# Handing a layer's token mixer to its channel mixer: the last tile by halves of 512, its neighbour turned inside the last product, the written order begun one tile earlier, and 13 sums a layer on GpSimd

## The chip, the cores and the metric

One core of a Trainium2 chip runs the whole kernel. The metric is device time in microseconds. The core has TensorE (PE; its weight loads are listed as PEld), VectorE (DVE), ScalarE (ACT), GpSimd (POOL) and SyncE (SP, which issues the transfers). A program runs one queue of instructions on each engine, and the engines wait for each other through semaphores.

## The reference

Two layers of an encoder over 1024 tokens of 1024 channels, all in float32. Cut to what matters here:

```python
def rms_norm(x, g):
    return x * rsqrt(mean(x * x, -1) + EPS) * g

def conv_glu_ffn(h, w_in, conv_w, conv_b, w_out):      # D_FF = 2816
    gate, val = split(h @ w_in, 2, -1)
    gate = conv over tokens, 3 taps, per channel (gate) + conv_b
    return (gelu(gate) * val) @ w_out

# layer i
y = mixer_i(rms_norm(x, g0))           # attention of the layer, ending in o @ w_o
x = x + rms_norm(o @ w_o, g1)          # g1: norm of the mixer's output
f = conv_glu_ffn(rms_norm(x, g2), ...)
x = x + rms_norm(f, g3)
x = x + gated embedding (x, p[i], g4)
```

Layer 0's mixer is a neighbourhood attention over 16 x 64 tokens, layer 1's a dense differential attention. The places that change are the two at which `o @ w_o` ends and `h @ w_in` begins.

## The kernel before

**Products in float32.** An operand is split into a high part (a rounding copy, `high`, by ScalarE, line 249) and a low part (what is left, `low`, by VectorE, line 252). A product of two operands is then three matmuls into one sum bank (`mm3`, lines 286 to 288): high by high, low weight by high, high weight by low.

**The mixer's last product.** `mix_out` goes over eight tiles of 128 tokens in the order 0, 4, 1, 5, 2, 3, 6, 7. For each tile it multiplies by w_o (48 matmuls, line 1392: eight blocks of 128 channels, two halves of 512 output channels, three matmuls each), and then:

- ScalarE squares the two halves of the result (1551), VectorE adds the two sums (1555), GpSimd raises the mean to the power -1/2 (298: "the root"), VectorE scales by the root and g1 (1561: "the residual") and adds x (1564);
- ScalarE squares the new x (293), GpSimd takes the second root (298), and VectorE scales by it and g2 (306, for the last tile 1605: "the norm");
- TensorE turns the tile (eight transposes, 317), and the parts are stored for the channel mixer.

The names below call the last four tiles c = 2, d = 3, a = 6 and b = 7. Tiles 0 to 3 are one half of the tokens and 4 to 7 the other.

**The channel mixer.** `h @ w_in` is worked in 22 blocks of output channels. A block's 2 x 2 product is formed in seven products instead of eight (the operands are named A for weights, B for tokens, S and T for their sums): one = A11 B11, six = S2 T2, two = A12 B21, three = S3 T3, five = S1 T1, four = A22 T4, seven = S4 B22. A product is twelve matmuls, and the results are summed by VectorE (`upper`, 1785, is one of these sums) and GpSimd (`upper_on`, 1788). The token sums are made per tile while it is turned: T1 = B12 - B11 (`sum_t1`, 1496), T2 = B22 - T1 (`sum_t2`, 1500), T3 = B22 - B12 (`sum_t3`, 1504) and T4 = B21 - T2 (`sum_t4`, 1508). The weights come as raw pages, and their sums S1 to S4 (`sum`, 1746; for the first two blocks lines 75 and 79) are made by VectorE up to block 4, from block 5 on by GpSimd. After every second block four sums Z (1914 to 1917) of the gated result are made by VectorE, for the product by w_out, and written out.

**The order.** The scheduler orders ScalarE and VectorE up to tile a. From the last tile on, to the end of the third block, their order is the written one (`manual_schedule`, ending after `first_three`); TensorE runs as written throughout. The last product does three of its eight channel blocks, then turns tile d, then does the other five; behind it stand tile a's transposes, block 0's `one`, block 1's `one`, `two` of block 0, tile b's transposes, `two` of block 1, and then `six`. `Begun` holds what blocks 0 and 1 need before the last token tile is there.

Of the kernel before, what the change touches and what calls it, by code (L numbers as in the profile page):

```python
# [40 lines left out]
class Begun:  # L41


    def __init__(self, trunk, layer, X):
        self.trunk, self.layer, self.X = trunk, layer, X
        self.A = [trunk.weights_of(layer, 0)]
        self.o = [{k: trunk.operand(self.A[0][k]) for k in ("A11", "A12")}, {}]
        self.begun = []

    def weight(self, f, k):  # L50
        self.o[f][k] = self.trunk.operand(self.A[f][k])

    def weights(self):
# [152 lines left out]
class Trunk:  # L206
# [1229 lines left out]
    def mix_out(self, layer, x_in, x1):  # L1436
# [9 lines left out]
        with ExitStack() as pools:  # L1446
            x = pools.enter_context(self.tc.tile_pool(name=f"xb{layer}", bufs=2, reuse_waits="tile"))
            if layer == 0:
                self.ps = pools.enter_context(self.psum("s", 2))
            else:  # L1450
                pools.push(self.spool)
# [77 lines left out]
            def product_of(n, t, amid=None):  # L1529
                hi, lo, xi = ready.pop(0)  # L1530
                part = [(hi[:, k], lo[:, k]) for k in range(KT)]
                if t == 0 or layer == 1 and n == 1:
                    m = (self.out1 if n else self.out0)[2]
                    self.times(m, part[KT - 1 :], W[KT - 1 :], first=False)
                else:
                    m = self.ps.tile([P, D], F32, tag="s", name=self.uid("m"))
                    m = [m[:, :512], m[:, 512:]]
                    if amid is None:
                        self.times(m, part, W)
                    else:  # L1540
                        for _ in self.times_steps(m, part[:3], W[:3], last=False):
                            pass
                        amid()
                        self.times(m, part[3:], W[3:], first=False)
                return m, xi

            def squares(m, h):
                ss = [self.col("ss"), self.col("sy")]
                for half in range(2):
                    w = slice(half * 512, half * 512 + 512)  # L1550
                    nc.scalar.activation(h[:, w], m[half], AF.Square, scale=D**-0.5, accum_out=ss[half])
                return ss
# [31 lines left out]
            m, xi = product_of(NT - 1, b, lambda: self.transposed(hs[-2], put(order[-3], hs[-2])))  # L1584
            h = self.page(x, "h")
            hs.append(h)
            (a1, a2), (b1, b2) = sums(hs[-2]), sums(h)
            ss = squares(m, h)
# [3 lines left out]
            gate.weights()  # L1592
            self.high(grid(ps[1]), of(b22, a))
            self.high(grid(ps[0]), of(b12, a))
            gate.one(0)
            residual(b, m, h, xi, r)
            self.split(a1, *both("T1", a))
            gate.copy(0)
            gate.one(1)
            sum_t2(a, a1, a2)  # L1600
            gate.weight(1, "A12")
            r = self.rstd(xi, h)
            gate.copy(1)
            gate.sum1(0), gate.sum2(0)
            nc.vector.scalar_tensor_tensor(out=h, in0=xi, scalar=r, in1=g2, op0=ALU.mult, op1=ALU.mult)
            s2 = gate.high(0, 1)
            self.high(a2, both("T2", a)[0])
            gate.low(0, 1, s2)
            gate.two(0)
# [61 lines left out]
    def product(self, ps, o, X, first):  # L1671
        for k in range(4):
            self.mm3(ps, (o[:, 0, k], o[:, 1, k]), (X[:, 0, k], X[:, 1, k]), first and k == 0, k == 3, not first)
# [4 lines left out]
    def gated(self, layer, X, spill, spare):  # L1678
# [38 lines left out]
        with self.tc.tile_pool(name=f"xd{layer}", bufs=1, reuse_waits="tile") as y, self.psum("c", 2) as pc:  # L1717
# [7 lines left out]
            class Block:  # L1725
# [33 lines left out]
                def product(b, ps, a, x, first):  # L1759
                    self.product(ps, b.o[a], X[x], first)  # L1760
# [8 lines left out]
                def six(b):  # L1769
                    b.product(b.pc, "S2", "T2", True)  # L1770
# [44 lines left out]
            def first_three():  # L1815
# [3 lines left out]
                b0.six()  # L1819
# [49 lines left out]
                b2.copy()  # L1869
                b0.gelu()  # L1870
                b2.centre(0)
                b0.mult((1,))
                b2.three(), b2.upper(), b2.upper_on(pool)
                b0.mult((0,))
                b1.taps(1)
# [4 lines left out]
                return b0, b1, b2  # L1880
# [3 lines left out]
            for f in range(FT):  # L1884
                if f < 3:
                    b = begun[f]
                else:
                    b = Block(f)
                    b.part("A11")
                    for s in ("S1", "S2", "S3", "S4"):  # L1890
                        b.sum(s, tt if f < 5 else pool)
                    b.part("S2", "A12", "S1", "S3", "S4", "A22")
# [21 lines left out]
                tt(out=Z[:, 0], in0=even[:, t2], in1=c[:, t2], op=add)  # L1914
                tt(out=Z[:, 1], in0=Z[:, 0], in1=even[:, t1], op=sub)
                tt(out=Z[:, 2], in0=even[:, t1], in1=even[:, t2], op=sub)
                tt(out=Z[:, 3], in0=c[:, t1], in1=Z[:, 1], op=sub)
# [502 lines left out]
```

## Time and profile before

| | |
|---|---|
| median of three runs | 2681.57 us (2681.15 to 2682.80) |
| the profiled execution | 2682.3 us, its span 2680.5 us |
| TensorE clock granted | 0.999 |
| busy PE, PEld | 2656.7 us (99%), 2198.9 us (82%) |
| busy DVE, ACT, POOL | 1964.7 us (73%), 1385.2 us (52%), 554.4 us (21%) |
| handover of layer 0, layer 1 | about 535 to 660 us, 1933 to 2057 us |

Rows of the timeline read: start, duration, engine, line, operation, output<-inputs, the shape, how many instructions were joined; in brackets the idle time before it and what ended it. In rows of windows a stretch is followed by each engine's busy time and count. Matmuls overlap by their pipeline, so two starts tell more than one duration.

### The profile page before, as it was taken

What the parts mean: (1) busy time and instruction counts of PE and PEld (TensorE: products, weight loads), DVE (VectorE), ACT (ScalarE), POOL (GpSimd) and SP (SyncE); (2) the same over time, 40 slices, a digit from 0 to 9 for tenths busy, and PEclk for the clock granted to TensorE, in tenths of its full rate; (3) what the DMA queues carried; (4) which work ended last, traced back from release to release, by engine and by line L of the source; (5) the groups of instructions that cost most, each with busy time, mean ns of one, the idle gap of its engine ahead of it and who ended that gap; (6) DMA issues with size and microseconds to landing.
All of it is one profiled execution on the core that took longest, in us unless ns stands there. A gap on an engine that the chain in (4) does not pass through costs nothing.

```text
span 2680.5 us, 37056 instructions
## 1 busy us (share of the span) xinstructions
PE 2656.7 (99%) x13428; PEld 2198.9 (82%) x13428; DVE 1964.7 (73%) x3369; ACT 1385.2 (52%) x2615; POOL 554.4 (21%) x528
## 2 busy tenths in 40 slices
PE   8999999999999999999999999999999999999999
PEld 7888887878888888888878888887878888888887
DVE  5777777699777778676587777775798777768674
ACT  5565556354444444454466666676454343444452
POOL 3221220003343300001442121210103433300000
PEclk9999999999999999999999999999999999999999
DMA  6323225523323274343346555553414232373443
GB/s 177 94 66 105 78 90 190 137 71 126 118 95 114 87 275 146 102 141 110 118 165 210 199 184 196 179 187 100 155 66 141 84 118 95 121 253 133 118 132 108
DMA packets 151081, 360.91 MB, mean 135 GB/s; under 512 B 14153, under 2 KB 41289, under 8 KB 150898
## 3 DMA queue, kind: packets, MB, share of 16 engines
q1 hardware_dynamic: 150898, 358.56, 40.9%
q8 instruction: 105, 1.72, 0.3%
q14 instruction: 78, 0.64, 0.1%
HBM read 277.79 MB, written 92.90 MB: 138 GB/s over the span
## 4 chain that ended last, share of the span: by engine, by line
PE 91%; DVE 4%; ACT 2%; issue 1%; DMA 1%; POOL 1%; SPq 0%; ACTq 0%; DVEq 0%; POOLq 0%
PE b L286 20%; PE b L288 20%; PE b L287 20%; PE m L1392 5%; PE g L1392 5%; PE b L1146 4%; PE s L1088 4%; PE b L1132 2%; PE b L1392 2%; PE b L317 2%; PE av L981 2%; PE b L954 1%; PE s L935 1%; PE s L934 1%; DVE r L252 1%
## 5 line engine op out<-in xcount | busy, mean ns | idle before, releaser
L286 PE MATMUL b<-r,ws 128*128 128x512 f32 x1244 | 512.8, 412 | 0.0
L288 PE MATMUL b<-r,ws 128*128 128x512 f32 x1244 | 487.4, 392 | 0.4 <-DVE ws L252 0.4
L287 PE MATMUL b<-r,ws 128*128 128x512 f32 x1244 | 486.7, 391 | 0.5 <-DVE r L252 0.5
L288 PEld LDWEIGHTS b<-r,ws 128*128 128x128 f32 x1244 | 233.5, 188 | 52.9 <-DVE ws L252 1.3
L298 POOL TENSOR_TENSOR ss<-ss,mhalf 128x1 f32<-128x1 f32 x128 | 77.7, 608 | 944.6 <-DVE ss L1150 416.4
L286 PEld LDWEIGHTS b<-r,ws 128*128 128x128 f32 x1244 | 234.1, 188 | 45.4 <-issue 2.9
L286 PE MATMUL b<-r,wa 128*128 128x512 f32 x688 | 268.0, 390 | 2.0 <-DVE B L1785 2.0
L288 PE MATMUL b<-r,wa 128*128 128x512 f32 x688 | 268.0, 389 | 0.0
L287 PE MATMUL b<-r,wa 128*128 128x512 f32 x688 | 267.7, 389 | 0.0
L287 PEld LDWEIGHTS b<-r,ws 128*128 128x128 f32 x1244 | 234.9, 189 | 34.7 <-DVE r L252 1.4
L286 PE MATMUL b<-r,r 128*128 128x512 f32 x648 | 254.4, 393 | 1.1 <-ACT ws L2161 0.6
L287 PE MATMUL b<-r,r 128*128 128x512 f32 x648 | 252.9, 390 | 0.0
L288 PE MATMUL b<-r,r 128*128 128x512 f32 x648 | 252.4, 390 | 0.0
L249 ACT ACTIVATE r<-raw 128x512 fp32r<-128x512 f32 (+1 forms) x168 | 108.8, 655 | 193.6 <-PE b L287 170.1
L252 DVE TENSOR_TENSOR ws<-raw,ws 128x512 fp32r<-128x512 f32 (+3 forms) x177 | 171.4, 974 | 47.1 <-ACT ws L249 45.4
L1102 DVE CUSTOM_DVE_ANT_0 E<-s,T 128x1024 f32<-128x1024 f32 x128 | 155.7, 1218 | 33.7 <-PE s L1088 32.9
L249 ACT ACTIVATE ws<-raw 128x512 fp32r<-128x512 f32 (+3 forms) x177 | 122.4, 698 | 110.3 <-PE b L288 51.9
L252 DVE TENSOR_TENSOR r<-raw,r 128x512 fp32r<-128x512 f32 (+1 forms) x168 | 125.1, 749 | 70.5 <-ACT r L249 66.3
L1392 PE MATMUL m<-r,ws 128*128 128x512 f32 x672 | 157.5, 392 | 0.0
L286 PEld LDWEIGHTS b<-r,wa 128*128 128x128 f32 x688 | 129.2, 188 | 29.9 <-DVE B L1785 3.3
L288 PEld LDWEIGHTS b<-r,wa 128*128 128x128 f32 x688 | 129.1, 188 | 27.8 <-DVE wa L252 1.0
L1109 ACT ACTIVATE E<-E,mn 128x1024 f32<-128x1024 f32 x128 | 146.9, 1148 | 9.6 <-DVE mn L1102 8.2
(235 smaller groups left out, 5528.1 us busy)
## 6 DMA issues: line engine op xcount, KB each, us to landing
r<-stashT SPq DMA_DIRECT2D x108, 512.0 KB, 4.9
raw<-in_w_in SPq DMA_DIRECT2D x86, 512.0 KB, 3.5
raw<-in_qkv SPq DMA_DIRECT2D x48, 512.0 KB, 4.3
spillS<-r SPq DMA_DIRECT2D x88, 256.0 KB, 3.2
r<-in_ffn_w_out SPq DMA_DIRECT2D x40, 512.0 KB, 6.2
raw<-spillS SPq DMA_DIRECT2D x40, 512.0 KB, 3.5
spillA<-B SPq DMA_DIRECT2D x66, 256.0 KB, 3.0
raw<-spillA SPq DMA_DIRECT2D x30, 512.0 KB, 3.7
```

The source lines that it names most:

```text
L249: return self.nc.scalar.activation(hi, src, AF.Copy).ins
L252: return self.nc.vector.tensor_tensor(out=lo, in0=src, in1=hi.bitcast(F32), op=ALU.subtract).ins
L286: mm(out, sta[0], mov[0], start=first, stop=False, skip_group_check=onto)
L287: mm(out, sta[0], mov[1], start=False, stop=False, skip_group_check=onto)
L288: mm(out, sta[1], mov[0], start=False, stop=last, skip_group_check=onto)
L298: self.nc.gpsimd.tensor_tensor(out=ss, in0=ss, in1=self.mhalf, op=ALU.pow)
L317: self.nc.tensor.transpose(t[:, k * P : k * P + P], h[:, c : c + P], self.ident)
L1088: nc.tensor.matmul(s[m][:, w], A[o, a, q], A[o, b, w], start=z == 0, stop=z == 2)
L1102: self.nc.vector.tensor_tensor_reduce(out=e, in0=s, in1=bias, scale=1.0, scalar=3e38, op0=ALU.add, op1=ALU.min, accum_out=mn)
L1109: self.exp = self.nc.scalar.activation(e, e, AF.Exp, bias=mn, scale=-1.0, accum_out=sm).ins
L1146: nc.tensor.matmul(o, wT[:, k], V[:, k], start=k == 0, stop=k == KT - 1)
L1392: mm(out[half], a, b[:, w], start=first and k + z == 0, stop=last and k == n - 1 and z == 2)
```

## The change

For each layer:

1. **Tiles.** The norms of tiles d and a, and the whole work of tiles a and b, come into the written order, which now also holds GpSimd. The last product is in steps: three channel blocks, tile d's transposes, one channel block, blocks 5 to 8 of half 0, blocks 5 and 6 of half 1, tile a's transposes, blocks 7 and 8 of half 1. Each half has a sum bank of its own; in layer 1 the fourth product takes the banks named `pj`.
2. **Halves.** Tile b's residual, addition, second square and norm are each done in halves of 512 channels.
3. **Weights.** Block 0's A11 and block 1's A12 are opened (high part) early and closed (low part) later; S1 and S2 of block 0 are summed, and A12 split, during the last product; block 3's A11, S1, S2 and A12 are worked inside `first_three`.
4. **GpSimd.** Five token sums (`sum_t2` of a, `sum_t3` of both, `sum_t4` of both) and the eight Z sums of blocks 1 and 3 go from VectorE to GpSimd.
5. **six.** Block 0's `six` does its eight matmuls with the high token part first, the four with the low part last.

The core of the diff:

```diff
-            for n, t in enumerate(order[:-1]):
+            for n, t in enumerate(order[:-2]):
...
-                self.normed(xi, h, g2)
-                if n + 2 < NT:
-                    ready.append(load(order[n + 2]))
+                if n < NT - 3:
+                    self.normed(xi, h, g2)
+                ready.append(load(order[n + 2]))
...
-            self.region = self.tc.manual_schedule(engines={ENG.Activation, ENG.DVE})
+            self.region = self.tc.manual_schedule(engines={ENG.Activation, ENG.DVE, ENG.Pool})
...
+            m, xb, steps = last_product(b)
+            steps(0, 3)
+            ps = [self.turned(hs[-2], g) for g in range(2)]
+            hs.append(self.page(x, "h"))
+            steps(3, 4)
...
+            r = self.rstd(xa, h)
+            self.low(grid(ps[1]), *both("B21", d))
+            gate.weights()
+            steps(4, 8, 0)
+            ss = [self.col("ss"), self.col("sy")]
+            square(m[0], hs[-1], 0, ss)
+            norm(h, xa, r, slice(0, D))
+            gate.sum1(0)
+            gate.sum2(0)
+            gate.weight(0, "A12")
+            steps(4, 6, 1)
+            ps = [self.turned(h, g) for g in range(2)]
+            steps(6, 8, 1)
...
+            square(m[1], h, 1, ss)
             sum_t1(a, ps[0], a1)
             r = root_of(ss)
...
+            sum_t2(a, a1, a2, pool)
...
+            for n, w in enumerate(halves):
+                nc.vector.scalar_tensor_tensor(
+                    out=h[:, w], in0=m[n], scalar=r, in1=g1[:, w], op0=ALU.mult, op1=ALU.mult
+                )
+                tt(out=xb[:, w], in0=h[:, w], in1=xb[:, w], op=ALU.add)
+                if n == 0:
+                    s2 = gate.high(0, 1)
+                square(xb[:, w], h, n, sy)
...
+            r = root_of(sy)
             gate.one(1)
+            gate.copy(1)
+            gate.close(1, "A12", A12)
+            gate.two(0)
+            sum_t3(a, pool)
+            norm(h, xb, r, halves[0]), norm(h, xb, r, halves[1])
             self.high(a2, both("T2", a)[0])
-            gate.low(0, 1, s2)
-            gate.two(0)
             ps = [self.turned(h, g) for g in range(2)]
             gate.two(1)
             sum_t1(b, ps[0], b1)
             self.high(grid(ps[1]), of(b22, b))
             self.high(grid(ps[0]), of(b12, b))
+            sum_t3(b, pool)
             sum_t2(b, b1, b2)
+            self.high(b2, both("T2", b)[0])
             self.low(a2, *both("T2", a))
-            self.split(b2, *both("T2", b))
+            self.low(b2, *both("T2", b))
+            self.split(a1, *both("T1", a))
             self.split(b1, *both("T1", b))
...
-                sum_t4(a, a2), sum_t4(b, b2)
-
-            sum_t3(a), sum_t3(b)
+                sum_t4(a, a2, pool), sum_t4(b, b2, pool)
...
+        if late:
+            steps = [(a, k, 0) for k in range(4) for a in (0, 1)] + [(0, k, 1) for k in range(4)]
...
-                b0.six()
+                b0.six(True)
...
+                b3 = Block(3)
+                b3.part("A11")
...
+                tz = pool if f < 4 else tt
+                tz(out=Z[:, 0], in0=even[:, t2], in1=c[:, t2], op=add)
```

How the order moves, in layer 0 (numbers tell one page or bank from another).

TensorE, the end of the last product. `m` is the sum before, `b_1037` half 1 of it after; `h_5537` and `h_5543` are tile a. Before:

```order
L1392 MATMUL m_5565<-r_896_4687,ws_5466 128x512 x2
L317 MATMUL b_1038_5634<-ident,h_5537 128x128 x4
L317 MATMUL b_1039_5639<-ident,h_5537 128x128 x4
L286 MATMUL b_1043_5657<-r_945_4957,ws_5557 128x512
L287 MATMUL b_1043_5657<-r_945_4957,ws_5557 128x512
```

After:

```order
L326 MATMUL b_1047_5640<-ident,h_5543 128x128 x4
L326 MATMUL b_1048_5645<-ident,h_5543 128x128 x4
L1401 MATMUL b_1037_5563<-r_896_4687,ws_5465 128x512
L1401 MATMUL b_1037_5563<-r_897_4688,ws_5465 128x512
L1401 MATMUL b_1037_5563<-r_896_4687,ws_5466 128x512
L1401 MATMUL b_1037_5563<-r_896_4687,ws_5465 128x512
L1401 MATMUL b_1037_5563<-r_897_4688,ws_5465 128x512
L1401 MATMUL b_1037_5563<-r_896_4687,ws_5466 128x512
L295 MATMUL b_1049_5662<-r_945_4957,ws_5560 128x512
```

Tile a's eight transposes moved ahead of the last six matmuls.

GpSimd, up to block 0's `upper_on` (before: both roots of tile a, both of tile b; after: those of tile b). `B_950`, `B_951` and `B_952` are the tokens' B12, B21 and B22, `h_5543` holds tile a's T2, `h_5592` tile b's. Before:

```order
L298 TENSOR_TENSOR ss_5538<-ss_5538,mhalf 128x1
L298 TENSOR_TENSOR ss_5548<-ss_5548,mhalf 128x1
L298 TENSOR_TENSOR ss_5630<-ss_5630,mhalf 128x1
L298 TENSOR_TENSOR ss_5694<-ss_5694,mhalf 128x1
L1788 TENSOR_TENSOR B_950_4970<-B_950_4970,c_1081_5996 128x512
```

After:

```order
L307 TENSOR_TENSOR ss_5625<-ss_5625,mhalf 128x1
L1506 TENSOR_TENSOR h_5543<-B_952_4972,h_5543 128x512
L307 TENSOR_TENSOR ss_5680<-ss_5680,mhalf 128x1
L1510 TENSOR_TENSOR B_950_4970<-B_952_4972,B_950_4970 128x64x8 x2
L1514 TENSOR_TENSOR B_951_4971<-B_951_4971,h_5543 128x64x8
L1514 TENSOR_TENSOR B_951_4971<-B_951_4971,h_5592 128x64x8
L1869 TENSOR_TENSOR B_950_4970<-B_950_4970,c_1089_6007 128x512
```

Five sums now stand between and behind the two roots, the first `sum_t3` (line 1510, joined with tile b's) right behind the second root.

VectorE, behind tile b's transposes: T2, the lows of T2, T1 and S1, and then the sums T3 and T4. `r_946` is T2, `r_948` T1, `r_945` B11, `ws` are weights. Before:

```order
L1500 TENSOR_TENSOR h_5629<-B_952_4972,h_5629 128x512
L252 TENSOR_TENSOR r_946_4958<-h_5537,r_946_4958 128x64x8
L252 TENSOR_TENSOR r_946_4958<-h_5629,r_946_4958 128x64x8
L252 TENSOR_TENSOR r_948_4960<-h_5629,r_948_4960 128x64x8
L252 TENSOR_TENSOR ws_5750<-r_1040_5648,ws_5750 128x512
L75 TENSOR_TENSOR r_1040_5648<-r_1040_5648 128x512
L79 TENSOR_TENSOR r_1040_5648<-r_1040_5648,raw_5649 128x512
L252 TENSOR_TENSOR ws_5755<-r_1040_5648,ws_5755 128x512
L252 TENSOR_TENSOR ws_5758<-r_1040_5648,ws_5758 128x512
L1504 TENSOR_TENSOR B_950_4970<-B_952_4972,B_950_4970 128x64x8 x2
L1508 TENSOR_TENSOR B_951_4971<-B_951_4971,h_5537 128x64x8
L1508 TENSOR_TENSOR B_951_4971<-B_951_4971,h_5629 128x64x8
```

After, from tile b's norm:

```order
L1608 SCALAR_TENSOR_TENSOR h_5592<-x_5471,ss_5680,g_959_4987 128x512 x2
L1502 TENSOR_TENSOR h_5592<-b_1056_5728,r_945_4957 128x512
L1502 TENSOR_TENSOR h_5592<-h_5592,r_945_4957 128x512
L1506 TENSOR_TENSOR h_5592<-B_952_4972,h_5592 128x512
L261 TENSOR_TENSOR r_946_4958<-h_5543,r_946_4958 128x64x8
L261 TENSOR_TENSOR r_946_4958<-h_5592,r_946_4958 128x64x8
L261 TENSOR_TENSOR r_948_4960<-h_5543,r_948_4960 128x64x8
L261 TENSOR_TENSOR r_948_4960<-h_5592,r_948_4960 128x64x8
L261 TENSOR_TENSOR ws_5763<-r_1042_5609,ws_5763 128x512
```

Tile a's low of T1 has come in ahead of S1's low (`ws`), and the sums of lines 1504 and 1508 have gone to GpSimd. The norm is two instructions.

More of the change, by code (lines that the diff above doesn't have):

```diff
@@ L1534, in product_of, with last_product, steps, square @@
                     self.times(m, part[KT - 1 :], W[KT - 1 :], first=False)
-                else:
+                elif layer == 1 and n == 2:
                     m = self.ps.tile([P, D], F32, tag="s", name=self.uid("m"))
                     m = [m[:, :512], m[:, 512:]]
[L1538 to L1544, printed above, removed]
-                return m, xi
+                    self.times(m, part, W)
+                else:
+                    m = [self.bank(sums_of) for _ in range(2)]
+                    self.times(m, part, W)
+                return m, xi
+            def last_product(t):
+                hi, lo, xi = ready.pop(0)
+                part = [(hi[:, k], lo[:, k]) for k in range(KT)]
+                m = [self.bank(sums_of) for _ in range(2)]
+                def steps(k0, k1, half=None):
+                    out, mov = m, W[k0:k1]
+                    if half is not None:
+                        w = slice(half * 512, half * 512 + 512)
+                        out, mov = m[half : half + 1], [(wh[:, w], wl[:, w]) for wh, wl in mov]
+                    for _ in self.times_steps(out, part[k0:k1], mov, k0 == 0, k1 == KT):
+                        pass
+                return m, xi, steps
+            def square(src, h, half, ss):
+                w = slice(half * 512, half * 512 + 512)
+                nc.scalar.activation(h[:, w], src, AF.Square, scale=D**-0.5, accum_out=ss[half])
             def squares(m, h):
@@ L1549, in squares @@
                 for half in range(2):
[L1550 to L1551 removed]
+                    square(m[half], h, half, ss)
                 return ss
@@ L1582, in mix_out @@
             self.region.__enter__()
-            a, b = order[-2:]
[L1584 to L1588, printed above, removed]
-            ps = [self.turned(hs[-2], g) for g in range(2)]
+            pool = nc.gpsimd.tensor_tensor
+            norm = lambda h, xi, r, w: nc.vector.scalar_tensor_tensor(
+                out=h[:, w], in0=xi[:, w], scalar=r, in1=g2[:, w], op0=ALU.mult, op1=ALU.mult
+            )
@@ new lines, in mix_out @@
+            halves = slice(0, 512), slice(512, 1024)
+            a, b = order[-2:]
+            c, d = order[-4:-2]
+            r = self.rstd(xi, h)
+            m, xa = product_of(NT - 2, a)
+            ps = [self.turned(hs[-2], g) for g in range(2)]
+            hs.append(self.page(x, "h"))
+            for g in range(2):
+                self.high(grid(ps[g]), both(("B11", "B21")[g], c)[0])
+            self.low(grid(ps[0]), *both("B11", c))
+            norm(h, xi, r, slice(0, D))
+            h = hs[-1]
@@ new lines, in mix_out @@
+            r = root_of(squares(m, h))
+            self.low(grid(ps[1]), *both("B21", c))
+            self.high(grid(ps[1]), of(b21, c))
+            residual(a, m, h, xa, r)
+            A11 = gate.open(0, "A11")
+            m, xb, steps = last_product(b)
+            steps(0, 3)
+            ps = [self.turned(hs[-2], g) for g in range(2)]
+            hs.append(self.page(x, "h"))
+            steps(3, 4)
+            for g in range(2):
+                self.high(grid(ps[g]), both(("B11", "B21")[g], d)[0])
@@ L1669, in operand, with product @@
         return o
-    def product(self, ps, o, X, first):
+    def product(self, ps, o, X, first, late=False):
+        if late:
+            steps = [(a, k, 0) for k in range(4) for a in (0, 1)] + [(0, k, 1) for k in range(4)]
+            for n, (a, k, b) in enumerate(steps):
+                self.nc.tensor.matmul(
+                    ps, o[:, a, k], X[:, b, k], start=first and n == 0, stop=n == 11, skip_group_check=not first
+                )
+            return
         for k in range(4):
```

93 lines of the change are left out of this document (53 added, 40 removed).

## The prediction

> **What bounds the kernel now.** I read the page's busy times first, then the waits of TensorE, then the two handovers (product w_o into channel mixer) row by row.
>
> ```profile
> PE 2656.7 (99%) x13428; PEld 2198.9 (82%) x13428; DVE 1964.7 (73%) x3369; ACT 1385.2 (52%) x2615; POOL 554.4 (21%) x528
> ```
>
> TensorE is the bound, and the change leaves its matmuls as many as they were, so only its gaps can move. The view of waits, TensorE alone (total, times, longest, us), has four rows for the handovers:
>
> ```profile
> PE b L317 <- DVE h L1605: 2.4, 2, 1.2
> PE b L286 <- DVE B L1785: 2.0, 3, 1.2
> PE b L287 <- DVE r L252: 0.5, 2, 0.2
> PE b L317 <- ACT B L249: 0.3, 2, 0.2
> ```
>
> That is 5.2 us in nine waits, over two layers. The timeline of layer 0's handover shows where they stand (start, us, engine, line, out<-in, count, idle and releaser):
>
> ```profile
> 540.59 0.60 PE L317 MATMUL b<-ident,h 128*128 128x128 f32 x4
> 541.34 0.66 PE L317 MATMUL b<-ident,h 128*128 128x128 f32 x4 [0.15 <-ACT B L249]
> 541.76 7.07 PE L1392 MATMUL m<-r,ws 128*128 128x512 f32 x30
> 548.83 1.06 PE L317 MATMUL b<-ident,h 128*128 128x128 f32 x8
> ...
> 557.71 0.39 PE L288 MATMUL b<-r,ws 128*128 128x512 f32 x1
> 559.29 1.06 PE L317 MATMUL b<-ident,h 128*128 128x128 f32 x8 [1.19 <-DVE h L1605]
> 560.11 0.48 PE L286 MATMUL b<-r,ws 128*128 128x512 f32 x1
> ...
> 562.95 0.44 PE L286 MATMUL b<-r,ws 128*128 128x512 f32 x1
> 563.61 0.50 PE L287 MATMUL b<-r,ws 128*128 128x512 f32 x1 [0.22 <-DVE r L252]
> 626.16 0.39 PE L288 MATMUL b<-r,wa 128*128 128x512 f32 x1
> 626.83 0.50 PE L286 MATMUL b<-r,wa 128*128 128x512 f32 x1 [0.29 <-DVE B L1785]
> 645.78 0.39 PE L288 MATMUL b<-r,wa 128*128 128x512 f32 x1
> 647.33 0.50 PE L286 MATMUL b<-r,wa 128*128 128x512 f32 x1 [1.16 <-DVE B L1785]
> ```
>
> Thirty matmuls from 541.76 to 548.83 give a pitch of 0.236; eight transposes take 0.82 (559.29 to 560.11). What the starts exceed these by is the true loss: 0.34 in the transposes at 540.59 (0.75 for four, against 0.41), 1.35 at 559.29, 0.43 at 563.61, 0.44 at 626.83, 1.32 at 647.33: 3.9 in layer 0, 0.18 a wait more than the idle column. Layer 1 has four of the nine, idle 5.2 - 3.0 = 2.2, so 2.9. **The most that can be saved is 6.8 us, 0.25%.** About 0.2% (5.4 us) is what a measurement of this kernel can tell from no change.
>
> The producer in these waits is VectorE; the windows show how full it is (span, then busy us and count of PE, PEld, DVE, ACT, POOL; clock, DMA share, GB/s):
>
> ```profile
> 580.00:600.00 20.00, 20.00 (x89) 16.27 (x88) 19.62 (x34) 11.43 (x20) 0.00 (x0) 1.00 0.20 60
> 700.00:720.00 20.00, 20.00 (x90) 16.54 (x89) 15.51 (x23) 8.29 (x13) 6.87 (x6) 1.00 0.33 118
> ```
>
> At the handover VectorE has 0.4 of 20 us free, in the steady state 4.5: here everything added to it arrives late at TensorE, and everything taken off it should help. That is what the 13 sums on GpSimd bear on.
>
> **A sum on GpSimd.** Rows of both engines where they meet already:
>
> ```profile
> 629.16 1.20 DVE L252 TENSOR_TENSOR wa<-r,wa 128x512 fp32r<-128x512 f32 x1
> 629.77 1.75 POOL L1746 TENSOR_TENSOR r<-raw,raw 128x512 f32<-128x512 f32 x1
> 630.89 2.88 DVE L1813 TENSOR_TENSOR B<-B,B 128x512 f32<-128x512 f32 x2
> 634.36 0.62 DVE L1697 SCALAR_TENSOR_TENSOR B<-u,convw,B 128x31 f32<-128x31 f32 x1
> 635.00 1.72 POOL L1746 TENSOR_TENSOR r<-raw,r 128x512 f32<-128x512 f32 x1
> 635.50 1.78 DVE L1916 TENSOR_TENSOR r<-B 128x512 f32<-128x512 f32 x1
> 651.90 1.29 POOL L1746 TENSOR_TENSOR r<-raw,r 128x512 f32<-128x512 f32 x1 [0.69 <-DVE wa L252]
> ```
>
> A sum alone takes GpSimd 1.29 (651.90). VectorE's like operation takes 0.68 at a pitch of 0.60 (below, 550.22 to 550.83). The one at 635.50, issued while GpSimd's ran, took 1.78: held 1.10. The four disturbed VectorE rows lose 0.52, 1.60 (2.88 for two), 0.38 and 1.10, together 3.6 to the five GpSimd operations of 627.9 to 636.7: 0.72 each, against the 0.60 that a sum frees. In a full stretch a sum on GpSimd therefore brings VectorE nothing on average, and 1.10 of delay where it begins just ahead.
>
> [...]
>
> **Part by part, per layer.** *Tile d's turn*: its second four transposes waited for a bank that ScalarE empties behind VectorE's work for this handover. Of that work the lows of two gate weights now come later: -0.34; at worst it stays, 0. The halves of 512 issue the same 36 matmuls in another order, at no cost on TensorE.
>
> *Tile a's turn* now stands six matmuls before the product's end, at 548.83 - 6 x 0.236 - 0.34 = 547.1. Its norm ends too late for that today:
>
> ```profile
> 547.40 1.28 DVE L306 SCALAR_TENSOR_TENSOR h<-x,ss,g 128x1024 f32<-128x1024 f32 x1 [0.73 <-POOL ss L298]
> ```
>
> It ends at 548.68. In the new order the lows of tile d (two of 0.60) stand behind tile a's residual addition instead of ahead of it, and one low of tile c less stands ahead of its root: 1.8 earlier, 546.9. Loss 0, on a margin of 0.2; at worst 1.2, if only the root's low is saved.
>
> *Tile b's turn.* The chain behind the last product now:
>
> ```profile
> 548.92 0.60 ACT L1551 ACTIVATE h<-m 128x512 f32<-128x512 f32 x1 [2.44 <-PE m L1392]
> 550.22 0.69 DVE L1496 TENSOR_TENSOR h<-h,r 128x512 f32<-128x512 f32 x1
> 550.83 0.21 DVE L1555 TENSOR_SCALAR ss<-ss,sy 128x1 f32<-128x1 f32 x1
> 551.18 0.86 POOL L298 TENSOR_TENSOR ss<-ss,mhalf 128x1 f32<-128x1 f32 x1 [3.82 <-DVE ss L1555]
> 552.08 1.41 DVE L1561 SCALAR_TENSOR_TENSOR h<-m,ss,g 128x512 f32<-128x512 f32 x2 [0.44 <-POOL ss L298]
> 553.52 1.23 DVE L1564 TENSOR_TENSOR x<-h,x 128x1024 f32<-128x1024 f32 x1
> 554.84 1.06 ACT L293 ACTIVATE h<-x 128x1024 f32<-128x1024 f32 x1 [1.03 <-DVE x L1564]
> 556.76 0.86 POOL L298 TENSOR_TENSOR ss<-ss,mhalf 128x1 f32<-128x1 f32 x1 [4.72 <-DVE ss L294]
> 557.25 0.69 DVE L79 TENSOR_TENSOR r<-r,raw 128x512 f32<-128x512 f32 x1
> 557.86 1.28 DVE L1605 SCALAR_TENSOR_TENSOR h<-x,ss,g 128x1024 f32<-128x1024 f32 x1
> 1331.29 0.55 POOL L298 TENSOR_TENSOR ss<-ss,mhalf 128x1 f32<-128x1 f32 x1 [12.57 <-DVE ss L1150]
> 1331.80 2.66 POOL L707 TENSOR_TENSOR r<-r,r 128x512 f32<-128x512 f32 x2
> ```
>
> From the product's end (548.83) to the second root's end (556.76 + 0.86 = 557.62) it takes 8.79. Off it come one square of 0.60 (half 0 is squared while half 1 is multiplied), the 0.61 that the root's addition waits for the T1 pair (550.22 to 550.83), and about 0.5 as residual, addition and square overlap by halves; sum_t2 on GpSimd beside half 0's addition gives back some 0.2. So 7.3. TensorE turns tile a ahead of the product's end, and comes 0.82 earlier as well: at 36 x 0.23 = 8.3. Half a norm (0.69) behind 7.3 would be in time within 0.1. But GpSimd's next operation begins 0.04 before a root's ends (1331.80 against 1331.84), VectorE's 0.04 after it (552.08 against 552.04). sum_t3(a), now queued right behind the second root, thus takes the memory first, and the norm's first half is held 1.10: ready at 9.2, the second at 9.8. Loss 1.15 instead of 1.35: -0.2. Bounds: not held, 0.1, so -1.25; held in both halves or behind another operation, 2.2, so +0.85. I take the hold, as both starts have rows.
>
> *The first six and five.* Behind tile b's transposes VectorE has eight operations (T1's pair, T2, four lows, S1's low; before seven), seven with two SBUF inputs. Without holds the last ends 0.66 + 8 x 0.61 + 0.1 = 5.6 after the transposes' start; TensorE wants it at 0.82 + 24 x 0.23 = 6.3, and T2's lows at 5.4, since the low halves now come last. In the same stretch stand sum_t3(b) and both sum_t4 on GpSimd: three holds, 3.3. T2's lows, behind two of them, then come at 5.9, 0.5 late; S1's, behind all three, at 8.9, where five, by then late itself, wants it from its third matmul, 6.3 + 0.5 + 0.5 = 7.3: 1.6 more. 2.1 lost where 0.43 is now, +1.67. Bounds: no hold, -0.43; a fourth hold, +2.5. I take three, as nothing on VectorE is left between them.
>
> *Block 3's and 4's upper sums* (626.83, 647.33). In the two orders VectorE has 89 instructions instead of 92 from block 0's S3 to the first of them, and 111 instead of 118 to the second: 1.8 and 4.2 saved at 0.60 each. GpSimd has four and seven Z sums by then, which hold it 4 x 0.72 = 2.9 and 7 x 0.72 = 5.0; TensorE itself comes about 1.0 later by the terms above. Net 0 (1.8 + 1.0 - 2.9 and 4.2 + 1.0 - 5.0 are -0.1 and +0.2); bounds -1.3 and +1.3, layer 0's larger gap gone or doubled.
>
> *At nothing*: the two residual squares by halves on ScalarE (two of 0.60 for one of 1.06, beside TensorE); the sum banks taken singly; block 3's first weights earlier (they fill stretches with VectorE's same operations); one load of raw weights changing places with a spill on SP's queue (it lands in microseconds, and is wanted tens later). Were that cover gone, it is one VectorE operation, 0.68, each.
>
> **Sum**: -0.34 + 0 - 0.2 + 1.67 + 0 = +1.13 a layer, +2.3 in all. The profiled execution took 2682.3, 0.7 above the median; so 2684.6 there and **2683.9** as a median. This case's own range, the terms' bounds combined as independent: 2679.5 to 2687.5.
>
> **Rivals.** *The holds miss the path.* If GpSimd's sums begin while VectorE works from PSUM or has just started, each costs VectorE little; tile b's loss falls to 0.1, six and five to 0, the upper sums gain 1.3. Per layer -0.34 - 1.25 - 0.43 - 0.9, in all near -6: 2675.6. For it: VectorE's longest waits go where it frees 0.60 a sum. Against: the four disturbed rows out of five. It counts as faster from 5.4 of the 6.8 saved.
>
> *Every sum is paid on the path* (slower). sum_t3(a) holds both halves of the norm, and sum_t3(b), sum_t4 and the Z sums each hold 1.10 with no slack: +0.85, +2.5, +0.5 - 0.34 = +3.5 a layer, +7: 2688.6. For it: 19.62 of 20 busy. Against: a GpSimd operation that loses a race waits itself (629.77, 1.75) and VectorE's row before it (629.16) shows only 0.52. It decides from five holds a layer that TensorE sees.
>
> **Numbers.** The forecast 0.67, holds off the path 0.17, all on it 0.16. Of the first 0.01 is beyond +0.2%; of the second 0.14 is below -0.2%, of the third 0.14 above: faster 0.14, same 0.71, slower 0.15. The range reaches to the middle of either rival, 2676.5 to 2688.5.
>
> **What would show it.** Right: no idle before tile d's second transposes; GpSimd's sum_t3 within 0.05 of the root's end, and the norm's first half at about 1.8 instead of 0.7; TensorE's idle before tile b's transposes near 1.0; a new wait of 1 to 2 us of five on L252's lows. Wrong: DVE rows of 0.69 beside GpSimd's sums; five without a wait; or waits in the later blocks, where block 3's parts moved, which I set to nothing.

## The result, and the profile after

The changed kernel is slower: its median is 2690.95 us (2690.07 to 2691.96, seven runs) against 2682.65 for the kernel before on the same chip, a ratio of 1.0033 with the interval 1.0021 to 1.0044. That is +8.3 us where +2.3 was forecast; 2690.95 lies above the range. The profiled execution has a span of 2688.7 us, 8.2 more than before.

The page's busy times, and the handovers' rows in the view of TensorE's waits, after:

```profile
PE 2658.3 (99%) x13428; PEld 2200.2 (82%) x13428; DVE 1974.1 (73%) x3347; ACT 1385.1 (52%) x2619; POOL 592.2 (22%) x554
```

```profile
PE b L295 <- DVE B L1866: 5.0, 2, 3.0
PE b L296 <- DVE r L261: 2.6, 3, 0.9
PE b L326 <- DVE h L1608: 1.7, 2, 0.9
PE b L295 <- DVE u L1854: 1.5, 3, 0.9
PE b L1749 <- DVE r L261: 1.1, 2, 0.5
```

VectorE has 22 instructions fewer and is busy 9.4 us longer: single instructions of it take longer beside GpSimd's, as the rows below show, and that counts as busy. The waits for the upper sums (L1866, before L1785) grew from 2.0 to 5.0, and rows for the lows of six and five (L1749, two of the three of L296) and for a block's sum u (L1854) are new. In TensorE's timeline of layer 0:

```profile
539.50 1.03 PE L326 MATMUL b<-ident,h 128*128 128x128 f32 x8
545.84 1.04 PE L326 MATMUL b<-ident,h 128*128 128x128 f32 x8
557.26 1.23 PE L326 MATMUL b<-ident,h 128*128 128x128 f32 x8 [0.85 <-DVE h L1608]
563.62 1.20 PE L1749 MATMUL b<-r,ws 128*128 128x512 f32 x4 [0.55 <-DVE r L261]
565.91 0.50 PE L296 MATMUL b<-r,ws 128*128 128x512 f32 x1 [0.87 <-DVE r L261]
625.91 0.39 PE L297 MATMUL b<-r,wa 128*128 128x512 f32 x1
629.27 0.50 PE L295 MATMUL b<-r,wa 128*128 128x512 f32 x1 [2.97 <-DVE B L1866]
```

Tiles d and a (539.50, 545.84) are turned with no wait. "By the starts" means, here and below, what the time from one start to the next exceeds the undisturbed pitch by, 0.23 us for a matmul of 512 columns (the starts at 625.23, 625.45, 625.68 and 625.91 in the changed kernel). By the starts, tile b loses 1.20, six 0.71, five 1.41, block 3's upper sum 3.13. GpSimd and VectorE at tile b, in their timelines:

```profile
554.45 0.86 POOL L307 TENSOR_TENSOR ss<-ss,mhalf 128x1 f32<-128x1 f32 x1 [3.09 <-DVE ss L1576]
555.28 1.28 POOL L1510 TENSOR_TENSOR B<-B,B 128x512 f32<-128x512 f32 x1
559.69 1.61 POOL L1510 TENSOR_TENSOR B<-B,B 128x512 f32<-128x512 f32 x1 [3.12 <-ACT B L258]
561.26 3.44 POOL L1514 TENSOR_TENSOR B<-B,h 128x512 f32<-128x512 f32 x2
```

```profile
555.35 2.43 DVE L1608 SCALAR_TENSOR_TENSOR h<-x,ss,g 128x512 f32<-128x512 f32 x2 [0.44 <-POOL ss L307]
560.06 5.80 DVE L261 TENSOR_TENSOR r<-h,r 128x512 fp32r<-128x512 f32 x4
```

T3 of tile a begins at 555.28, 0.03 before the root ends; the norm's halves follow 0.07 behind it and take 2.43 together. The four lows take 5.80 with three sums beside them. Ahead of block 3's upper sum the timelines of VectorE and GpSimd have these rows:

```profile
603.00 0.69 DVE L261 TENSOR_TENSOR ws<-raw,ws 128x512 fp32r<-128x512 f32 x1 [0.56 <-ACT ws L258]
605.37 0.69 DVE L1894 TENSOR_TENSOR B<-B,B 128x512 f32<-128x512 f32 x1 [1.08 <-ACT B L1890]
610.90 1.91 DVE L1778 SCALAR_TENSOR_TENSOR B<-u,convw,B 128x480 f32<-128x480 f32 x2
621.87 0.90 DVE L1778 SCALAR_TENSOR_TENSOR B<-u,convw,B 128x31 f32<-128x31 f32 x1
623.29 1.78 DVE L261 TENSOR_TENSOR ws<-r,ws 128x512 fp32r<-128x512 f32 x1
625.78 1.00 DVE L1827 TENSOR_TENSOR r<-raw,r 128x512 f32<-128x512 f32 x1
628.54 0.68 DVE L1866 TENSOR_TENSOR B<-b,B 128x512 f32<-128x512 f32 x1
```

```profile
610.51 1.62 POOL L2005 TENSOR_TENSOR r<-B 128x512 f32<-128x512 f32 x1 [1.88 <-ACT ws L258]
621.43 1.28 POOL L2003 TENSOR_TENSOR r<-B 128x512 f32<-128x512 f32 x1 [9.30 <-DVE B L1894]
622.79 1.73 POOL L2004 TENSOR_TENSOR r<-r,B 128x512 f32<-128x512 f32 x1
624.60 1.63 POOL L2006 TENSOR_TENSOR r<-B,r 128x512 f32<-128x512 f32 x1
```

Four Z sums (L2003 to L2006) hold the four VectorE rows beside them. And VectorE stands idle, full as it is, for 0.56 for a weight's high part and for 1.08 until block 0's gelu is there (L1890), before it can multiply by it (L1894). At the same place before (line 1809 is the gelu, 1813 the product) it had:

```profile
600.34 1.28 DVE L252 TENSOR_TENSOR ws<-raw,ws 128x512 fp32r<-128x512 f32 x2
...
605.11 0.69 DVE L1813 TENSOR_TENSOR B<-B,B 128x512 f32<-128x512 f32 x1 [0.30 <-ACT B L1809]
```

### The profile page after: what moved, and what is told of

Its sections match the earlier page's. It is cut to its first block, busy times and chain, and to the rows that moved or that the text cites. A ratio compares the mean times of both kernels' runs of the same rounds, so it can differ in the third digit from the quotient of the medians.

```text
span 2688.7 us, 37071 instructions
## 1 busy us (share of the span) xinstructions
PE 2658.3 (99%) x13428; PEld 2200.2 (82%) x13428; DVE 1974.1 (73%) x3347; ACT 1385.1 (52%) x2619; POOL 592.2 (22%) x554
## 4 chain that ended last, share of the span: by engine, by line
PE 90%; DVE 5%; ACT 2%; issue 1%; DMA 1%; POOL 1%; SPq 0%; ACTq 0%; DVEq 0%; POOLq 0%
PE b L295 20%; PE b L297 20%; PE b L296 20%; PE b L1401 7%; PE g L1401 5%; PE b L1155 4%; PE s L1097 4%; PE b L1141 2%; PE b L326 2%; PE av L990 2%; PE b L963 1%; DVE r L261 1%; PE m L1401 1%; DVE B L1778 1%; PE s L944 1%
## 5 line engine op out<-in xcount | busy, mean ns | idle before, releaser
L296 PE MATMUL b<-r,ws 128*128 128x512 f32 x1236 | 484.0, 392 | 1.8 <-DVE r L261 1.7
L297 PEld LDWEIGHTS b<-r,ws 128*128 128x128 f32 x1236 | 232.2, 188 | 53.4 <-DVE ws L261 2.1
L295 PEld LDWEIGHTS b<-r,ws 128*128 128x128 f32 x1236 | 232.9, 188 | 48.3 <-issue 2.9
L296 PE MATMUL b<-r,wa 128*128 128x512 f32 x688 | 267.9, 389 | 0.0
L296 PEld LDWEIGHTS b<-r,ws 128*128 128x128 f32 x1236 | 233.6, 189 | 35.9 <-DVE r L261 3.0
L296 PE MATMUL b<-r,r 128*128 128x512 f32 x648 | 253.1, 391 | 0.9 <-DVE r L261 0.9
L1401 PE MATMUL b<-r,ws 128*128 128x512 f32 (+1 forms) x840 | 193.0, 387 | 0.5 <-ACT ws L2250 0.5
L1401 PEld LDWEIGHTS b<-r,ws 128*128 128x128 f32 x840 | 152.8, 188 | 30.4 <-ACT ws L2250 0.9
L295 PEld LDWEIGHTS b<-r,wa 128*128 128x128 f32 x688 | 129.2, 188 | 32.5 <-DVE B L1866 5.8
```

Of the source, the lines that this page charges most:

```text
L295: mm(out, sta[0], mov[0], start=first, stop=False, skip_group_check=onto)
L296: mm(out, sta[0], mov[1], start=False, stop=False, skip_group_check=onto)
L297: mm(out, sta[1], mov[0], start=False, stop=last, skip_group_check=onto)
L1401: mm(out[half], a, b[:, w], start=first and k + z == 0, stop=last and k == n - 1 and z == 2)
```

## The experiments

All were timed beside the kernel before. All but two of those in the table have 10 or 11 runs (the change has seven, z_dve six), and all lie within 2.4 us of their median; differences under 1 us between two versions tell nothing. In the table, + is slower than the kernel before in the same session. "Token sums" are the five of tiles a and b; "block 3's parts" are its A11, S1, S2 and A12, which the change wrote into `first_three`.

| version | token sums | Z sums | block 3's parts | median, us | to before |
|---|---|---|---|---|---|
| the change | GpSimd | GpSimd | as written | 2690.95 | +8.3 |
| tokens_dve | VectorE | GpSimd | as written | 2685.91 | +4.1 |
| z_dve | GpSimd | VectorE | as written | 2689.68 | +7.9 |
| b3_back | GpSimd | GpSimd | back | 2687.68 | +5.9 |
| sums_dve | VectorE | VectorE | as written | 2684.90 | +3.4 |
| z_dve_b3_back | GpSimd | VectorE | back | 2684.47 | +3.0 |
| tokens_dve_b3_back | VectorE | GpSimd | back | 2682.27 | +0.9 |
| sums_dve_b3_back | VectorE | VectorE | back | 2679.15 | -2.6 |

**Three parts taken back, one at a time and together.** The edits:

```diff
# tokens_dve: each of these without pool; T2(a) ahead of gate.close(1, "A12", A12), T3 behind the lows
-            sum_t2(a, a1, a2, pool)
-            sum_t3(a, pool)
-            sum_t3(b, pool)
-                sum_t4(a, a2, pool), sum_t4(b, b2, pool)
# z_dve
-                tz = pool if f < 4 else tt
+                tz = tt
# b3_back: no b3 in first_three, and in the loop again
+                    b = begun[f] if f < 3 else Block(f)
# sums_dve_b3_back: all three
```

> The changed kernel with its five token sums back on VectorE (T2 of tile a between the second root and the norm, T3 and T4 behind the lows as before). Theory 'held' (each GpSimd sum that starts ahead holds VectorE 1.1 us): the norm of tile b is two times 0.6 to 0.7, TensorE's loss before tile b's transposes falls from 1.2 to about 0.2, six and five lose under 0.5 instead of 2.1, so TensorE is 2.9 earlier there; VectorE gains 4.4 of holds and pays 3.0 for the sums, so block 3's upper sum comes only 1.4 earlier and its stall grows by 1.5: net -1.4 a layer, 2688. Rival 'local' (block 3's stall stays as it is): -2.9 a layer, 2685. Rival 'sums are neutral on VectorE': 2691.

> The changed kernel with the eight Z sums of a layer back on VectorE. Theory 'held' with the measured holds: at block 3 three Z sums cost 1.4 of holds on GpSimd and would cost 1.8 on VectorE, so block 3's stall stays (3.1 in layer 0, 2.2 in layer 1, within 0.6) and block 4's grows by up to 1: 2690 to 2693. Rival 'the Z sums are what made block 3 late': stalls back to 0.5, 2686.

> The changed kernel with block 3's A11, S1, S2 and A12 back behind the third block, where the scheduler places them. Theory 'ScalarE' (block 3's first weights, written ahead of block 0's gelu, make VectorE wait 0.56 for a weight's high part and 1.08 for the gelu, against 0.30 before): those waits go, block 3's stall falls by 1.3 a layer: 2688. Rival 'held alone': the stall stays, 2691, or grows because the same work now comes later, 2692.

> The changed kernel with all 13 sums on VectorE and block 3's parts back: what is left is tile d and a's earlier turn, the halves, the gate weights' places and six with its low part last. If the holds and the wait for ScalarE are all that cost time: tile d -0.34, tile b -1.2, six and five -0.3 a layer against the kernel before, 2679. If VectorE's work at blocks 3 and 4 takes back what the tiles gain: 2682 to 2683. If something else in the change costs time: 2685 or more.

Tokens_dve came out at the rival "local": tile b, six and five wait no more, and block 3's stall stayed at 3.13 and 2.15, as in the change. It did not grow, because VectorE came earlier and waited for the gelu all the same (1.08). In z_dve block 3's stall fell to 0.56 in layer 0 and 1.44 in layer 1, which the first theory had excluded, but in layer 0 TensorE then lost 1.32 to a copy by ScalarE (L1845), which stands behind block 2's gelu, and 2.56 to block 4's upper sum. The time is only 0.4 to 1.3 lower (by the difference to before, by the median): the loss moved. B3_back gave 2.4 to 3.3, about the 3 expected, but at block 3 it gave more than the 1.3 expected: the upper sum in layer 0 loses 0.67 instead of 3.13. All three together gave 2679.15, the 2679 expected if these costs are all there is, and beat the kernel before: ratio 0.9990 (0.9981 to 0.9999). So what is left of the change, the tile order, the halves, the gate weights' places and six, does bring time, taken together. One wait is new in it: in product `three` of block 0 TensorE loses 0.98 a layer to T3's low part, called T3's wait below. In this version's timeline of VectorE the norm and the four lows are:

```profile
555.30 1.41 DVE L1608 SCALAR_TENSOR_TENSOR h<-x,ss,g 128x512 f32<-128x512 f32 x2
...
559.10 2.68 DVE L261 TENSOR_TENSOR r<-h,r 128x512 fp32r<-128x512 f32 x4
```

They take 1.41 against 2.43, and 2.68 against 5.80: the same instructions, held 1.02 and 3.12 with GpSimd's sums beside them.

**Each part alone.** Versions with two of the three taken back (edits as above).

> The changed kernel with all 13 sums on VectorE, block 3's first parts left where the change wrote them. It shows what these parts cost alone. Theory 'ScalarE': VectorE's wait for the gelu and for A11's high part remains and nothing else, up to 1.5 us a layer above the version with everything back (2679.15): 2682. If the costs of the three parts simply add: 2690.95 - 5.0 - 1.3 = 2684.6. If block 3's parts cost nothing without GpSimd's sums beside them: 2679.

> The changed kernel with the Z sums on VectorE and block 3's parts back, the five token sums left on GpSimd. Theory 'held': tile b 1.2 and six and five 2.1 a layer come back, T3's wait of 1.0 goes, block 3's and 4's stalls as in the version with everything back: 2679.15 + 2 x 2.3 = 2683.8. Rival 'absorbed' (VectorE, the bound to block 4, does as much work either way): 2680.

> Only the eight Z sums of a layer stay on GpSimd; token sums on VectorE, block 3's parts back. With the token sums on GpSimd they cost 3.2 (2687.68 against 2684.47), with block 3's parts early 1.0 (2685.91 against 2684.90). Theory 'held': they hold VectorE ahead of block 3's and 4's upper sums whatever the tiles do, +3.2: 2682.4. Rival 'they cost only where VectorE is late already': 2680.

Over 2679.15, by the differences to before: the token sums alone cost 5.6 (two layers of 1.20 at tile b and 2.1 at six and five are 6.6, less T3's wait of 1.0 a layer that goes: 4.6), the Z sums 3.5, block 3's parts 6.0. They don't add up: they are 15.1 apart, 10.9 together (the last section comes back to this). For the token sums the theory "held" was right in its waits too: they are those of the change at tile b, six and five, T3's wait is gone, and the upper sums lose what they lose with everything back. For the Z sums "held" was met in number only, which is luck. From block 3 on TensorE loses 1.52 in layer 0, where with everything back it loses 1.75; in layer 1 it loses 3.84 instead of 0.72, in one wait of 2.24 for a block's sum u (L1854) and in 1.40 at half clock behind it. For block 3's parts "ScalarE" was too small, and 2684.6 by addition was met without a reason.

**One sum at the root.** As sums_dve_b3_back, with `sum_t3(a, pool)` ahead of tile b's norm.

> Everything back as in the version of 2679.15 but one sum a layer: T3 of tile a on GpSimd, right behind the second root. Theory 'the order at the root': it begins before VectorE's norm of tile b, whose first half takes 1.8 instead of 0.7, TensorE loses 1.0 before tile b's transposes, T3's wait shrinks by 0.6 at most: 2679.15 + 2 x (0.4 to 1.0) = 2680 to 2681. Rival 'VectorE is first, or GpSimd waits': norm halves of 0.7, 2678 to 2679.

It took 2680.27, 1.1 to 1.4 above the version it starts from. Its timelines of GpSimd, VectorE and TensorE:

```profile
554.06 0.86 POOL L307 TENSOR_TENSOR ss<-ss,mhalf 128x1 f32<-128x1 f32 x1 [4.34 <-DVE ss L1576]
554.89 1.38 POOL L1510 TENSOR_TENSOR B<-B,B 128x512 f32<-128x512 f32 x1
```

```profile
555.03 2.46 DVE L1608 SCALAR_TENSOR_TENSOR h<-x,ss,g 128x512 f32<-128x512 f32 x2
```

```profile
556.97 1.23 PE L326 MATMUL b<-ident,h 128*128 128x128 f32 x8 [0.76 <-DVE h L1608]
```

No other of the 13 sums is on GpSimd here. VectorE was at work until the norm, the sum began 0.03 before the root's end, and the norm is held 1.05 (2.46 against 1.41). That shows the mechanism at tile b by itself.

**Work put into a wait.** As sums_dve_b3_back, with `sum_t4(a, a2)` behind `gate.sum1(1), gate.sum2(1)`; and the same with `b0.six()` for `b0.six(True)`.

> Everything back as in the version of 2679.15, and T4 of tile a summed in VectorE's 0.70 us wait for the high parts of block 1's S pages instead of ahead of T3's lows. If VectorE's backlog sets the wait of product three (0.98 by the starts in both layers), it shrinks by 0.6: 2678. If the wait in the gap is only moved, 2679.

> The fastest version so far (2678.19) with block 0's six in its old order, each low token part right behind the high one. T2's low of tile b ends 3.0 after the transposes' start by its rows, six begins 3.6 after it and wants a low from its third matmul: if so it does not wait, 2678.2. If the low is later than that, it loses up to 0.4 a layer, 2679.

With T4 in the gap it took 2678.19, ratio 0.9988 (0.9979 to 0.9997): the fastest version, and 3.3 under the kernel before. T3's wait went from 0.98 to 0.38 by the starts, the 0.6 expected if VectorE's backlog sets it. With six in its old order it took 2678.75, which can't be told from 2678.19. Its timeline has a new wait in six, 0.36 a layer by the starts, but the 0.38 that were left of T3's wait are gone: the loss only changed its place, and no worth of six's order is shown here.

**Why block 3's parts cost so much.** First by halves (sums on VectorE; A11 alone early, or S1, S2 and A12 alone).

> All sums on VectorE; of block 3's parts only A11 stays where the change wrote it, ahead of block 0's gelu. All parts early cost 5.8 (2684.90 against 2679.15). Theory 'ScalarE first' (A11's high part ahead of the gelu delays what VectorE waits for): most of it stays, 2683 or more. Rival 'VectorE's written work' (S1, S2 and A12 ahead of block 1's and 2's taps make the gelu of block 2, and behind it on ScalarE block 4's copy, late): 2680 or less.

> All sums on VectorE; of block 3's parts S1, S2 and A12 stay where the change wrote them, A11 is back. Theory 'VectorE's written work': 2683 or more. Theory 'ScalarE first': 2680 or less.

They took 2683.84 and 2683.04. Each theory was met in one run and refuted in the other: A11 alone costs 4.7 and the rest alone 3.9, of the 5.8 of all. In both VectorE waits for the gelu, 1.29 and 1.32. The order of VectorE's instructions then showed what had been taken for granted: block 3's weights did not come earlier. Before, the scheduler, which may slip work from behind the written stretch into it, had put both lows of A11 and A12 ahead of block 0's product; the change, by writing them, moved A12's low behind it. VectorE with everything back, and then sums_dve (`ws` from the raw page of block 3, `B_952<-B_952,B_950` the product by the gelu):

```
L261 TENSOR_TENSOR ws_6150<-raw_6146,ws_6150 128x512
L261 TENSOR_TENSOR ws_6160<-raw_6146,ws_6160 128x512
```

```
L261 TENSOR_TENSOR ws_6078<-raw_6074,ws_6078 128x512
L1827 TENSOR_TENSOR r_1042_5609<-raw_6076 128x512
L1894 TENSOR_TENSOR B_952_4972<-B_952_4972,B_950_4970 128x16x32
...
L261 TENSOR_TENSOR ws_6104<-raw_6074,ws_6104 128x512
```

The product by the gelu in their timelines, again everything back and then sums_dve:

```profile
602.69 0.69 DVE L1894 TENSOR_TENSOR B<-B,B 128x512 f32<-128x512 f32 x1 [0.27 <-ACT B L1890]
```

```profile
602.54 0.69 DVE L1894 TENSOR_TENSOR B<-B,B 128x512 f32<-128x512 f32 x1 [1.08 <-ACT B L1890]
```

Three runs test this:

```diff
# a12_ahead, from sums_dve
                 b2.part("S3")
+                b3 = Block(3)
+                b3.part("A11", "A12")
                 b1.taps(0)
...
-                b3 = Block(3)
-                b3.part("A11")
...
-                b3.part("A12")
# b3_as_scheduled: also
-                b3.sum("S1")
+                b3.sum("S1"), b3.sum("S3")
                 b0.mult((1,))
...
-                b3.part("S2")
                 b0.mult((0,))
+                b3.part("S2")
# before_b3_early: the kernel before, with block 3's lines of the change in first_three and the loop
```

> As the version with all sums on VectorE and block 3's parts where the change wrote them (2684.90), but A11 and A12 of block 3 written two steps earlier, ahead of block 1's taps, where the scheduler had put their low parts when it was free to. Theory 'the written place takes a low away from ahead of the gelu' (VectorE runs up to block 0's product with the gelu one low too soon, waits 1.08 instead of 0.27, and does the low afterwards, on the path of the upper sums): the wait falls to 0.3, 2679.5 to 2681. Rival 'the early parts themselves cost time, wherever they stand' : 2684 to 2685.

> The same, and S3's sum beside S1's ahead of that product, S2's parts behind its second half: up to there the order of VectorE's instructions is that of the version with block 3's parts back (2679.15). Theory 'the written place': 2679 to 2680. Rival 'a written order for block 3 costs time behind this place too': 2682 or more.

> The kernel before, with nothing changed but block 3's A11, S1, S2 and A12 written where the change has them. Theory 'the written place': VectorE's wait for the gelu grows from 0.30 to 1.1 to 1.3 and the time by 4 to 6, 2686 to 2687. Rival 'it costs time only beside the earlier tiles, which bring VectorE there 0.7 sooner': 2682 to 2683.

Before_b3_early took 2688.11, +6.6: the part costs its time without the tiles and without a sum on GpSimd moved, so the rival falls. VectorE's wait for the gelu, and where TensorE pays for it in layer 0:

```profile
603.74 0.69 DVE L1813 TENSOR_TENSOR B<-B,B 128x512 f32<-128x512 f32 x1 [1.08 <-ACT B L1809]
```

```profile
634.68 0.50 PE L286 MATMUL b<-r,ws 128*128 128x512 f32 x1 [1.13 <-ACT B L1764]
648.28 0.50 PE L286 MATMUL b<-r,wa 128*128 128x512 f32 x1 [2.35 <-DVE B L1785]
```

TensorE waits for ScalarE's copy behind block 2's gelu (L1764), and at block 4's upper sum 2.35 instead of 1.16; behind that it loses 1.4 more at half clock. Block 0's gelu, for which VectorE waits, starts 64.0 us after tile d's turn, hardly later than before (63.4). Block 2's gelu starts at 94.4 instead of 88.1: VectorE's last taps for it now stand behind block 3's upper sum (624.35), among sums that GpSimd makes in either kernel (L1788, L1746), and are held (0.71 and 0.74 undisturbed):

```profile
626.15 1.75 DVE L1697 SCALAR_TENSOR_TENSOR B<-u,convw,B 128x480 f32<-128x480 f32 x1
631.22 1.78 DVE L1697 SCALAR_TENSOR_TENSOR B<-u,convw,B 128x512 f32<-128x512 f32 x1
```

So in layer 0 the wait for the gelu marks the changed order; most of the loss is what that order does further on. A12_ahead took 2681.94, b3_as_scheduled 2682.01: about 3 of the 5.8 come back, and the wait for the gelu goes. So the written place costs about half of it. Both runs move A11 and A12 together; which of the two matters more, they don't tell. VectorE in b3_as_scheduled:

```profile
596.33 1.29 DVE L261 TENSOR_TENSOR ws<-raw,ws 128x512 fp32r<-128x512 f32 x2
...
601.72 0.69 DVE L1894 TENSOR_TENSOR B<-B,B 128x512 f32<-128x512 f32 x1
```

The other 2.8 stay. Up to the product the order is that of the version with everything back; behind it, it is not, and in layer 1 blocks 3 and 4 lose 1.3 by the starts instead of 0.7. Its runs go from 2679.69 to 2682.48, and its profile is of the fastest, with a span of 2677.9 like that of the version with everything back (2677.8). But its first 100 us took 1.0 less in that execution; its two handovers, from tile d's turn on, took 1.1 more. In layer 0 block 2's gelu starts 88.1 after tile d's turn, against 86.7 there. Where the rest of the 2.8 lies is open.

## Why the prediction was wrong, step by step

- **Tile d's and tile a's turn**: right. Forecast -0.34 and 0; measured 0 lost at both, from 0.40 and 0.16.
- **Tile b's turn**: right in place and size. Forecast a loss of 1.15 with T3 of tile a beginning within 0.05 of the root's end; measured 1.20.
- **Six and five**: right. Forecast 2.1 lost, measured 2.12 in layer 0 (0.71 + 1.41) and 2.10 in layer 1, on the same instructions.
- **Block 3's and 4's upper sums, "Net 0"**, and **"At nothing: block 3's first weights earlier"**: the two terms that failed. Together TensorE loses 5.2 more from block 3 on, against 0: in layer 0 block 3 lost 2.69 more (3.13 instead of 0.44) and block 4 gave back 1.0; in layer 1 the four waits of the blocks are 4.2 by the starts instead of 0.7.
- **How the 2.69 come about.** Counted from tile d's turn (540.59 before, 539.50 after), TensorE reached the place 0.84 later (626.16 and 625.91), about the 1.0 credited. But VectorE too came later to block 0's S3, by 0.37 (570.41 and 569.69): the sums that held its lows, and with them TensorE, had held VectorE itself. That the forecast left out. From there to the upper sum (626.10 and 628.54) VectorE took 3.16 more. Three instructions less are 1.8, as forecast. Four Z sums were put at 2.9 of holds, and the four rows of 610.90 to 625.78 give 1.04 + 0.66 + 1.10 + 0.32 = 3.12 (against 0.87, 0.24, 0.68 and 0.68 undisturbed). The rest is VectorE's idle time, 2.37 instead of 0.84, mostly the waits of 0.56 and 1.08 for ScalarE that block 3's parts brought; 0.3 remain unassigned. So in layer 0 "Net 0" was off by about 1.2, within its bounds, and "At nothing" by 1.5. B3_back agrees: with block 3's parts back TensorE loses 1.50 from block 3 on in layer 0, against 1.76 before. In layer 1 it loses 2.40 against 0.72, beyond the bound of 1.3, so there "Net 0" fails by itself.
- **What "At nothing" had wrong.** Block 3's parts were costed as work moved forward, with a price of 0.68 each if its cover went. A12's low was work moved back behind a wait, since the scheduler had had it earlier still. The parts cost 6.6 by themselves on the kernel before and 6.0 on the version with everything else back. The order of the two kernels, compared at block 0's product, would have shown it; moving A11 and A12 back to where the scheduler had them regained about half of that cost. The prediction's own sign for this, waits in the later blocks, is what came (629.27).
- **The total.** From the turn of tile d to 700 us, and in layer 1 to 2100, the same matmuls come 2.5 and 4.9 later, 7.5 of the 8.2 in span. The first three lines make about +2.0 of it, where the forecast for them was +2.3, the blocks 5.2. The first 100 us (-1.1) and the stretches outside the handovers (+1.8) are the rest, and they differ as much between other versions.
- **The rivals**: "every sum is paid on the path", 2688.6, was the nearest in time and has half of the cause. With block 3's parts back the 13 sums cost 5.9 + 2.6 = 8.5 together over sums_dve_b3_back, where it had +7; it lacked block 3's parts. "The holds miss the path" is refuted at tile b by t3a_gpsimd, and for the token sums by z_dve_b3_back. What the change brings without sums and block 3, 2.6, is far less than the 6 given there, because the upper sums keep their 2.5 and T3 waits.

The prediction's hold of 1.10, from the row at 635.50, stood up where VectorE began just behind a sum. In six rows where VectorE began second, it was held for 0.13 to 0.19 less than GpSimd's sum still had to run: at tile b 1.02 of 1.21, in t3a_gpsimd 1.05 of 1.24, and in the four rows beside Z sums 1.04 of 1.23, 0.66 of 0.84, 1.10 of 1.23 and 0.32 of 0.45. Of what the prediction calls taking the memory the runs show these holds, and that rows of VectorE with an input from a sum bank kept their usual time inside a sum of GpSimd's: 0.68 at 631.44 (the sum from 630.93 to 632.68) and 0.69 at 649.10 (648.57 to 650.31) in the changed kernel.

## What to carry to other kernels

A sum moved from a full VectorE to GpSimd frees 0.60 there, and beside it VectorE was held 0.7 to 1.1 in most of these places. One place for it stands out as bad: right behind a tiny GpSimd operation for which VectorE waits (1.05 of hold at tile b's norm in t3a_gpsimd). A place at which VectorE works on inputs from a sum bank may be better: one such operation took its usual 0.73 beside a sum (637.16 in the changed kernel, inside GpSimd's 1.29 from 636.77), but no run here tried to place a sum so. Before one writes an order out, one should look where the scheduler had put that work: to write it can mean to delay it. And where a sum credits that the consumer comes later, it has to ask whether the producer comes later for the same reason.

## What the runs showed of the hardware that was not expected

After some waits of TensorE its granted clock was about half for some 3 us (below from 627.29 to 630.38). TensorE's timeline in tokens_dve, and its windows:

```profile
623.92 0.39 PE L297 MATMUL b<-r,wa 128*128 128x512 f32 x1
627.29 0.79 PE L295 MATMUL b<-r,wa 128*128 128x512 f32 x1 [2.97 <-DVE B L1866]
627.88 0.63 PE L296 MATMUL b<-r,wa 128*128 128x512 f32 x1
628.31 0.63 PE L297 MATMUL b<-r,wa 128*128 128x512 f32 x1
```

```profile
627.00:630.50 3.50, 3.21 (x8) 2.59 (x9) 3.50 (x5) 0.89 (x1) 3.12 (x2) 0.53 0.42 146
631.00:640.00 9.00, 9.00 (x41) 7.44 (x41) 8.96 (x12) 2.76 (x5) 5.61 (x4) 1.00 0.18 58
```

The granted clock (the third number from the end) is 0.53 in the window behind the wait and 1.00 again from 631; the starts are 0.43 apart instead of 0.23, which cost 1.5 more. The same wait of 2.97 in the changed kernel was followed by full clock:

```profile
629.00:632.50 3.50, 3.23 (x14) 2.70 (x15) 3.50 (x5) 0.89 (x1) 3.14 (x2) 1.00 0.42 155
```

Of ten waits from 1.86 to 2.97 us in the handovers of all profiles, six were followed by half clock. All six are in versions with the token sums on VectorE; the four at full clock are in versions with them on GpSimd. Whether that is more than chance is open, and no run shows what decides between half and full clock.

So sums_dve, a11_early, before_b3_early, tokens_dve and tokens_dve_b3_back each carry 1.4 to 3.1 us of half clock in their profiled executions. That bears on the missing additivity. In these profiles the two handovers cost, over sums_dve_b3_back, 4.4 with the token sums alone, 3.7 with the Z sums alone and 6.2 with block 3's parts alone: 14.4 apart, and 10.2 in the change, which has no half clock. Without the half clock (1.4 in the second and 1.5 in the third) the parts are 11.5, so in these executions most of what doesn't add up is half clock. That is one execution of each, and no run took the half clock away by itself.
